# Attention units' scores and values set beside sample visits in a hybrid decoder step, with a later store and one subtraction moved between engines

## The chip, the cores and the metric

One core of a Trainium2 chip runs the whole step. The metric is the device time of one execution in microseconds. The engines are TensorE (PE in the profile; PEld is its loading of weights), VectorE (DVE), ScalarE (ACT), GpSimd (POOL) and SyncE (SP), which issues most of the DMAs. PE writes to PSUM, where an accumulator takes one of eight banks.

## The reference, cut to what matters

One layer of a decoder for a prompt of 1024 tokens and for 8 samples of 4 tokens, model width 1024. Two branches, each fed by the same projection, are joined by sigmoid gates:

```python
h, gate = adaln_in(x, c, w_ada, b_ada, g_norm)
(mq, mk, mv, mi, mf, mo, mz, aq, ak, av, az, gm, ga) = split_in(h @ w_in)
y_m, C, n, m = mlstm_branch(mq, mk, mv, mi, mf, mo, mz, C0, n0, m0, b_i, b_f, g_mn)
...
y_a = o.astype(x.dtype) * jax.nn.silu(az)          # o: sliding-window attention with sinks
u = jax.nn.sigmoid(gm) * (y_m @ w_mo) + jax.nn.sigmoid(ga) * (y_a @ w_ao)
x = x + gate * (u @ w_o)
```

The attention has 8 query heads in 2 groups of 64 channels and a window of 128 tokens: in blocks of 128 queries, scores against two blocks of keys, a softmax with a sink, and the values. The mLSTM branch goes through the prompt in chunks of 128 with a matrix memory per head; `m_p`, one of the outputs, is the last running maximum of its gates. The samples need the same projections, attention over a cache and an update of the matrix memories.

## The kernel before, in words

Nearly all of PE's time goes into the projections. A float32 product is made as three products of rounded parts (high times high, high times low, low times high). The first jobs are plain: 384 columns at a time, tiles `g_aq`, `g_mq` and so on. After the *plain jobs* come pairs of jobs as Strassen-like blocks (`block_products`, line 1698): seven products per pair, each of 12 matmuls of 512 columns, into the tiles `bx`, `bz`, `by` and `bw`. The attention's output projection has the same form (`AttPair` and `att_products`, lines 1840 and 1912; tiles `ax`, `az`, `ay`, `aw`).

All smaller work is put between these matmuls. `Side` (line 113) is the planner: it keeps a clock of its own, `side.now`, that each matmul advances by a modelled time, and streams of generators. A generator yields the time until its next step and the PSUM banks that the step needs (`a`, `b`, `o`; two of each). `tick` (line 140), called between matmuls, takes the steps that are due; a step that needs a bank only comes at a *visit*, when some time has passed since the last one (line 147). `HOLD` (line 110) says how long a step keeps a bank in this plan. PE's instructions stand in the order in which the program gives them; those of DVE and ACT are ordered by the framework's scheduler after the plain start, and each engine works through its own queue.

The streams that matter here:

- `unit(g, b0)` (line 931): one *attention unit*, two blocks of 128 queries of one group. It loads `uqk` and `uqv`, makes the scores (`sc`, in banks `o` behind the plain jobs, line 1166), their maxima and exponentials on DVE and ACT, the transposes of the probabilities (`pt`), and leaves its values to `values_now` (line 1013), which makes the tile `oT`, copies it to `p` on ACT and stores it to `oD` by POOL's queue. Before the change a unit that scores makes all waiting values first.
- `head(h)` (line 1181): an mLSTM head, with visits `tk`, `tv`, `S`, then `U`, `n`, and `ty`. `sample_head(h)` (line 1318): the samples of a head, with `stk`, `sS`, `sn`, `sU`, `st`, `sty`.
- *Sample visits*: once per pair, at the seventh or second block product, the samples' own projection is made from the raw weights: `samples_end` transposes the last pair's sums (`smpo`) and `samples` multiplies for the next pair (`smp`). Behind these the program calls `values_now` and a forced `tick` (lines 1781 and 1782). `smpo`, `smp` and `pt` use banks `b`.
- `gates` (line 668): the gates' maxima. Line 744 issues the store of `m_p` from `mn` as soon as the scan that makes `mn` is written. SP's queue is in order: a DMA that waits for its source holds those behind it. `store` and `due` (line 265) keep a store back until `side.now` has reached a given time.
- `AttPair.split` (line 1893): a weight block's high part is cast on ACT, its low part subtracted on DVE, except for blocks 3 and 4 of the first pair, which POOL subtracts (line 1902).

Of the kernel before, what the change touches and what calls it, by code (L numbers as in the profile page):

```python
# [10 lines left out]
F32 = mybir.dt.float32  # L11
# [4 lines left out]
ALU = mybir.AluOpType  # L16
# [90 lines left out]
JOBS = {n: i for i, n in enumerate(job_columns()[0])}  # L107


HOLD = {"a": 2.0, "b": 2.0, "o": 4.0, "+": 0.0}  # L110


class Side:
# [4 lines left out]
    def __init__(self, each, limits, quiet):  # L118
        self.each, self.free = each, {}
        self.now, self.last, self.quiet, self.products, self.left = 0.0, 0.0, quiet, 0, 99  # L120
        self.streams = {n: {"max": m, "gap": g, "wait": [], "live": [], "next": 0.0} for n, (m, g) in limits.items()}

    def add(self, stream, gen, banks=""):
# [16 lines left out]
    def tick(self, visit=False, then=None):  # L140
        self.each()
        for st in self.streams.values():
            if st["wait"] and len(st["live"]) < st["max"] and self.now >= st["next"]:
                self.begin(st)
        held, used = [], set()
        self.taken = False
        visit = visit or self.now >= self.last + self.quiet
        for item in sorted((i for st in self.streams.values() for i in st["live"]), key=lambda i: i[1]):
            banks = set(item[2])
            if self.now < item[1] or used & banks or (banks and not visit) or any(self.now < self.free.get(b, 0) for b in banks):  # L150
                continue
            used |= banks
            for b in banks:
                self.free[b] = self.now + (6.0 if "+" in banks else HOLD[b])
            if item[3]:
                held.append((item, self.now))
                self.now += 0.11 * item[3]
                continue
            n = self.products
            self.step(item)  # L160
            if self.products > n:
                self.last = self.now
        if then:
            then()
        now = self.now
        for item, self.now in held:
            self.step(item)
            self.last = max(self.last, self.now)
        self.now = now
# [17 lines left out]
def body(tc, a):  # L187
    nc = tc.nc
    with ExitStack() as ctx:
# [73 lines left out]
        due = []  # L263
# [404 lines left out]
        def gates(gp, zg, bias):  # L668
# [72 lines left out]
            V.tensor_tensor(d1, d1, bl, op=ALU.add)  # L741
            mn = cp.tile([1, 32], F32, name="mn")
            V.tensor_tensor_scan(mn, d0, d1, 0.0, ALU.add, ALU.max)
            dma(a["m_p"], mn.rearrange("p (h c) -> p h c", c=8)[:, :, 7])
            mr = cp.tile([1, 64], F32, name="mr")
            V.memset(mr[:, 32:33], 0.0)
            V.tensor_copy(mr[:, 33:64], mn[:, 0:31])
# [183 lines left out]
        def unit(g, b0):  # L931
            sink = at["sink"]
            los = [128 if b == 0 else 0 for b in (b0, b0 + 1)]
            n0 = 1 if b0 == 0 else 0
            qk, qv = ht([128, 4, 128], "uqk"), ht([128, 4, 128], "uqv")
            kT = qk[:, 1:4].rearrange("p c e -> p (c e)")
            q = qk[:, 0], qv[:, 0]
            vn = qv[:, 1], qv[:, 2], qv[:, 3]
            dma(kT[:, n0 * 128:], kD[:, (b0 - 1 + n0) * 128:(b0 + 2) * 128])
            for i in range(2):  # L940
                dma(q[i], qD[g][:, (b0 + i) * 128:(b0 + i + 1) * 128])
            dma(qv[:, 1 + n0:4], vnD[:, b0 - 1 + n0:b0 + 2])
            yield 12.0, sc_bank[1]
            values_now(pb if "+" in sc_bank[1] else po)
            p = [ht([128, 2, 256], f"p{kv}") for kv in range(2)]
            mx = sm([128, 4], "mx", 3)
            side.taken |= "+" in sc_bank[1]
            scs = [sc_bank[0]([128, 2, 256], f"sc{g}_{b0}_{kv}") for kv in range(2)]
            for i, lo in enumerate(los):
                kc = slice(i * 128 + lo, i * 128 + 256)  # L950
                for kv, r in enumerate(half_rows):
                    mm(scs[kv][:, i, lo:], q[i][r], kT[r, kc], start=True, stop=True, share=2)
            for kv in range(2):
                for i, lo in enumerate(los):
                    V.tensor_tensor_reduce(p[kv][:, i, lo:], scs[kv][:, i, lo:], amask[:, lo:], 1.0, sink[:, kv, g:g + 1],
                                           ALU.add, ALU.max, accum_out=mx[:, 2 * kv + i:2 * kv + i + 1])
            nmx = sm([128, 8], "nmx", 3)
            V.tensor_scalar(nmx[:, 0:4], mx, -1.0, None, op0=ALU.mult)
            v2 = lambda t: t.rearrange("p (k i) -> p k i", i=2)
            V.tensor_tensor(v2(nmx[:, 4:8]), sink[:, :, g:g + 1].to_broadcast((128, 2, 2)), v2(mx), op=ALU.subtract)  # L960
            yield 2.5, ""
            t0 = side.now
            yield from clear()
            den = sm([128, 4], "den", 3)
            S.activation(nmx[:, 4:8], nmx[:, 4:8], AF.Exp)
            for kv in range(2):
                for i, lo in enumerate(los):
                    j = 2 * kv + i
                    S.activation(p[kv][:, i, lo:], p[kv][:, i, lo:], AF.Exp, bias=nmx[:, j:j + 1],
                                 accum_out=den[:, j:j + 1])  # L970
            yield max(0.0, t0 + 3.0 - side.now), ""
            t0 = side.now
            yield from clear()
            V.tensor_tensor(den, den, nmx[:, 4:8], op=ALU.add)
            V.reciprocal(den, den)
            for kv in range(2):
                for i, lo in enumerate(los):
                    j = 2 * kv + i
                    if kv:
                        S.activation(p[kv][:, i, lo:], p[kv][:, i, lo:], AF.Copy, scale=den[:, j:j + 1])  # L980
                    else:
                        V.tensor_scalar(p[kv][:, i, lo:], p[kv][:, i, lo:], den[:, j:j + 1], None, op0=ALU.mult)
            yield max(0.0, t0 + 7.6 - side.now), "b", 2 * (4 - n0)
            pT = [t.rearrange("p i (j e) -> p (i j) e", e=128) for t in p]
            for kv in range(2):
                pt = (pb, pb if side.taken else po)[kv]([128, 4, 128], f"pt{g}_{b0}_{kv}")
                for j in range(n0, 4):
                    tr(pt[:, j], p[kv][:, j // 2, j % 2 * 128:j % 2 * 128 + 128], ident)
                if kv:
                    V.tensor_copy(pT[kv][:, n0:], pt[:, n0:])  # L990
                else:
                    S.copy(pT[kv][:, n0:], pt[:, n0:])
            yield 5.0, "o"
            due_values.append((g, b0, n0, vn, pT, p[0]))
            side.now = unit_products(n0)
            side.products += 2 * (4 - n0)
            units_done.append((g, b0))
# [15 lines left out]
        def values_now(pool=po):  # L1013
            joins_now()
            was, n = side.now, side.products
            side.taken |= pool is po and len(due_values) > 0
            for g, b0, n0, vn, pT, home in due_values:
                oT = pool([128, 2, 128], f"oT{g}_{b0}")
                for j in range(n0, 4):
                    i, hf = divmod(j, 2)  # L1020
                    for kv in range(2):
                        r = slice(64 * kv, 64 * kv + 64)
                        mm(oT[r, i], vn[i + hf][:, r], pT[kv][:, j], start=(hf == 0 or b0 + i == 0), stop=(hf == 1))
                c0 = b0 * 128
                o = home[:, 0]
                S.copy(o, oT.rearrange("p c e -> p (c e)"))
                issue(oD[g][:, c0:c0 + 256], o, eng=nc.gpsimd)
            due_values.clear()
            side.now, side.products = was, n

        def queries(g):
# [111 lines left out]
        def head_jobs(h):  # L1143
# [15 lines left out]
            for n, dst, smp, scale in (("mq", q, qs, float(128 ** -0.5)), ("mk", k, ks, 1.0), ("mv", v, vs, 1.0)):  # L1159
# [3 lines left out]
                if i == -1:  # L1163
                    plain_ends.append(True)
                    side.finish("g")
                    sc_bank[:] = po, "o+"
                    side.streams["a"]["max"] = 3
                    next(work)
                job((n, h), keep(dst, smp, scale, "s"), (lambda: next(work)) if i == -1 else None)
# [11 lines left out]
        def head(h):  # L1181
# [128 lines left out]
            if h == 2:  # L1310
                at["n0"], at["n1"] = (cp.tile([128, NH, NB], F32, name=n) for n in ("n0", "n1"))
                dma(at["n0"], a["state_n"])
                for i in range(NH):
                    side.add("s", sample_head(i), "ob")

        tails = []

        def sample_head(h):
            an, sxb, fls, wes = st["an"], st["sxb"], st["fls"], st["wes"]
            z = ht([128, 512], "sz")  # L1320
            kn = sm([96, 128], "skn", 1, F32R)
# [55 lines left out]
                    G.tensor_scalar(c, c, sxb[:, h, 2, b:b + 1], None, op0=ALU.mult)  # L1377

            joins.append(states)
            yield 4.0, "o"  # L1380
            settle(states)
            yield 4.0, "ob"
            for i, (c, b, m) in enumerate(zip(Cs, bs, ns_)):
# [314 lines left out]
        def block_products(jobs, hook):  # L1698
# [27 lines left out]
            for j, (n, i) in enumerate(flat):  # L1726
# [45 lines left out]
                if i == (2 if n else 7) and nxt:  # L1772
# [4 lines left out]
                        side.now += nxt.cost  # L1777
                    else:
                        nxt.samples()
                    values_now()  # L1780
                    side.free["b"] = side.now + HOLD["b"]
                    side.tick(True, values_now)
                    if nxt.kind in (head_in, gate):
                        nxt.first_sums()
                if i == 7 and nxt and nxt.kind not in (head_in, gate):
# [54 lines left out]
        class AttPair:  # L1840
# [52 lines left out]
            def split(self, i):  # L1893
# [5 lines left out]
                hi, lo = self.w[i] = [x[:, o:o + 2] for x in self.g[home]]  # L1899
                with behind(S, self.landed if i == 1 else []):  # L1900
                    S.copy(hi, t)
                (G if (self.i, i) in ((0, 3), (0, 4)) else V).tensor_tensor(lo, t, hi.bitcast(F32), op=ALU.subtract)
                if i == 2:
                    V.tensor_tensor(r0[:, 2:4], r0[:, 2:4], r0[:, 0:2], op=ALU.subtract)

# [757 lines left out]
```

## Time and profile before

| | us |
| --- | --- |
| time, three runs | 811.42, 811.79, 813.1 (median 811.79) |
| the profiled execution: its time, its span | 811.34, 809.6 |
| busy PE, PEld | 796.6, 668.8 |
| busy DVE, ACT, POOL | 600.7, 418.5, 82.3 |

The span goes from the first to the last instruction. The granted clock of TensorE is 0.999 over the span. In the profile's lines a row of the timeline reads: start, duration, engine, line, operation, out<-in, shape, count, and in brackets the idle time ahead with what ended it. A matmul's duration reaches past the start of the next, since they are pipelined; the distance between two starts is the time that one costs. Each float32 matmul of a visit leaves two records.

### The profile page before, as it was taken

The page shows a single profiled execution, that of the slowest core. Times are in us where ns is not written, and L with a number is a line of the kernel's source. Part 1 is how long each engine was busy: PE and PEld are TensorE (multiplying, and loading weights), DVE is VectorE, ACT ScalarE, POOL GpSimd, SP SyncE. Part 2 cuts the span into 40 slices and gives each one's busy share as a digit, 9 for nine tenths or more (in the row PEclk, how much of TensorE's full clock was granted, in tenths as well). Part 3 has the DMA queues.
Part 4 walks back from the last instruction along what each step waited for, and adds up shares of the span by engine and source line. Part 5 has one row for each costly group of instructions (what it writes and reads, how often), then busy time and mean ns, then how long its engine had stood idle before and what let it go on. Part 6 is the DMA issues. An engine that isn't in the chain of part 4 may idle for free.

```text
span 809.6 us, 15159 instructions
## 1 busy us (share of the span) xinstructions
PE 796.6 (98%) x5156; PEld 668.8 (83%) x5156; DVE 600.7 (74%) x1499; ACT 418.5 (52%) x1019; POOL 82.3 (10%) x158
## 2 busy tenths in 40 slices
PE   8999999999999999999999999999999999999996
PEld 5779888998788888888888888888888779996785
DVE  4899997647656466476657888998678998865776
ACT  5664346656474574556556655554446552224335
POOL 0120000010000000000001441330003201000000
PEclk9999999999999999999999999999999999999999
DMA  9994855556545425537655695675246599649322
GB/s 348 362 352 154 262 176 178 184 177 212 157 150 171 139 85 163 192 101 255 244 191 182 240 278 208 226 253 171 83 156 211 164 302 390 220 164 335 124 105 111
DMA packets 113794, 165.51 MB, mean 204 GB/s; under 512 B 21248, under 2 KB 55936, under 8 KB 113684
## 3 DMA queue, kind: packets, MB, share of 16 engines
q1 hardware_dynamic: 107316, 152.21, 56.9%
q10 hardware_dynamic: 4752, 7.60, 2.5%
q0 software_dynamic: 1648, 4.72, 1.5%
q8 instruction: 41, 0.67, 0.3%
q14 instruction: 37, 0.30, 0.1%
HBM read 115.51 MB, written 50.00 MB: 204 GB/s over the span
## 4 chain that ended last, share of the span: by engine, by line
PE 89%; DVE 5%; DMA 3%; issue 1%; ACT 1%; SPq 0%; DVEq 0%; ACTq 0%
PE by L296 13%; PE bw L296 12%; PE bx L296 12%; PE bz L296 6%; PE g_w_mo L296 6%; PE g_mq L296 3%; PE foW L296 3%; PE foY L296 2%; PE foX L296 2%; PE smp L296 2%; PE oT L296 2%; PE n L296 2%; PE g_ak L296 2%; PE sc L296 2%; PE pt L301 1%; PE g_mk L296 1%
## 5 line engine op out<-in xcount | busy, mean ns | idle before, releaser
L233 DVE CUSTOM_DVE_ANT_0 p<-sc,cst,sink 128x256 f32<-128x256 f32 (+1 forms) x64 | 26.3, 462 | 12.3 <-PE sc L296 11.1
L233 ACT ACTIVATE p<-p,nmx 128x256 f32<-128x256 f32 (+1 forms) x64 | 30.9, 484 | 8.3 <-DVE nmx L233 8.3
L233 POOL TENSOR_SCALAR Cs<-Cs,sxb 128x129 f32<-128x129 f32 x32 | 29.2, 930 | 45.7 <-PE sn L296 45.7
L296 PE MATMUL g_aq<-h_h,wh_aq 128*128 128x384 f32 (+1 forms) x96 | 31.9, 332 | 0.0
L296 PE MATMUL g_aq<-h_h,wl_aq 128*128 128x384 f32 (+1 forms) x96 | 30.9, 321 | 0.0
L296 PE MATMUL g_aq<-h_l,wh_aq 128*128 128x384 f32 (+1 forms) x96 | 30.8, 321 | 0.0
L296 PE MATMUL g_w_mo<-ym_h,wh_w_mo 128*128 128x384 f32 (+1 forms) x96 | 30.8, 321 | 0.0
L296 PE MATMUL g_w_mo<-ym_l,wl_w_mo 128*128 128x384 f32 (+1 forms) x96 | 30.8, 321 | 0.0
L296 PE MATMUL g_w_mo<-ym_l,wh_w_mo 128*128 128x384 f32 (+1 forms) x96 | 30.8, 321 | 0.0
L233 ACT CAST wosh<-wor 128x512 fp32r<-128x512 f32 x24 | 14.8, 622 | 13.8 <-DVE wor L233 13.8
L282 POOL DMA_DIRECT2D oD<-p x16 | 8.7, 544 | 130.1 <-ACT p L233 120.3
L233 DVE TENSOR_TENSOR wosl<-wor,wosh 128x512 fp32r<-128x512 f32 x24 | 16.7, 695 | 3.4 <-ACT wosh L233 2.6
L233 DVE COPY p<-pt 128x512 f32<-128x512 f32 (+1 forms) x16 | 10.5, 654 | 11.7 <-PE pt L301 11.6
L296 PEld LDWEIGHTS g_aq<-h_h,wh_aq 128*128 128x128 f32 x96 | 18.0, 188 | 1.0 <-issue 1.0
L233 DVE SCALAR_TENSOR_TENSOR tgw_mo<-tgw_mo,g_w_mo 128x384 f32<-128x384 f32 (+1 forms) x24 | 12.4, 518 | 8.1 <-PE g_w_mo L296 7.3
L296 PEld LDWEIGHTS g_w_mo<-ym_l,wl_w_mo 128*128 128x128 f32 x96 | 18.0, 188 | 0.1
L296 PEld LDWEIGHTS g_w_mo<-ym_l,wh_w_mo 128*128 128x128 f32 x96 | 18.0, 188 | 0.0
L296 PEld LDWEIGHTS g_aq<-h_l,wh_aq 128*128 128x128 f32 x96 | 18.0, 188 | 0.0
L296 PEld LDWEIGHTS g_w_mo<-ym_h,wh_w_mo 128*128 128x128 f32 x96 | 18.0, 188 | 0.0
L296 PEld LDWEIGHTS g_aq<-h_h,wl_aq 128*128 128x128 f32 x96 | 18.0, 188 | 0.0
L233 DVE TENSOR_TENSOR et<-et,S 128x384 f32<-128x384 f32 (+1 forms) x12 | 6.1, 510 | 15.8 <-PE S L296 15.8
L233 ACT ACTIVATE p<-p,den 128x256 f32<-128x256 f32 (+1 forms) x32 | 14.8, 491 | 3.8 <-DVE dec L233 2.1
(2072 smaller groups left out, 2837.7 us busy)
## 6 DMA issues: line engine op xcount, KB each, us to landing
early_h<-w_ada SPq DMA_DIRECT2D x8, 512.0 KB
adar_ga<-w_ada SPq DMA_DIRECT2D x16, 256.0 KB
wr_ga<-w SPq DMA_DIRECT2D x16, 256.0 KB
wr_gm<-w SPq DMA_DIRECT2D x16, 256.0 KB
taD<-gt SPq DMA_DIRECT2D x16, 256.0 KB
tmD<-gt SPq DMA_DIRECT2D x16, 256.0 KB
wor<-w_out SPq DMA_DIRECT2D x16, 256.0 KB
tga<-taD SPq DMA_DIRECT2D x16, 256.0 KB
```

Source lines behind the costliest of these rows:

```text
L233: ins = f(*args, **kw)
L282: ins = (eng or nc.sync).dma_start(out, in_)
L296: in_order(nc.tensor.matmul(out, lhsT, rhs, start=start, stop=stop, skip_group_check=more))
L301: in_order(nc.tensor.transpose(out, in_, idn))
```

## The change

It has three parts.

*Units and sample visits.* Behind the plain jobs a unit's scores now ask for a bank `!`, which `tick` gives only while `side.beside` is set, that is in the forced tick of a sample visit; they also must be free 3.5 us ahead by the plan. Values of at most two units at a time are made, into one tile, behind the scores of the same visit (in banks `b`) or, where there are none, as before in a bank `o`. Sample heads begin 8 to 17 us behind a sample visit, and their state products wait for the next one for up to 20 us. As the order of PE stands, PE has the same 3863 rows in all.

*The store of `m_p`* becomes due 14 us later on the planner's clock.

*Block 3 of the first attention pair* is subtracted on DVE instead of POOL.

```diff
-HOLD = {"a": 2.0, "b": 2.0, "o": 4.0, "+": 0.0}
+HOLD = {"a": 2.0, "b": 2.0, "o": 4.0, "+": 0.0, "!": 0.0}
...
+        self.beside, self.scored, self.turn = False, False, 0.0
...
-            if self.now < item[1] or used & banks or (banks and not visit) or any(self.now < self.free.get(b, 0) for b in banks):
+            if "!" in banks and not self.beside:
+                continue
+            now = self.now + 3.5 * ("!" in banks)
+            if now < item[1] or used & banks or (banks and not visit) or any(now < self.free.get(b, 0) for b in banks):
                 continue
...
-            dma(a["m_p"], mn.rearrange("p (h c) -> p h c", c=8)[:, :, 7])
+            due.append((side.now + 14.0, a["m_p"], mn.rearrange("p (h c) -> p h c", c=8)[:, :, 7]))
...
             yield 12.0, sc_bank[1]
-            values_now(pb if "+" in sc_bank[1] else po)
+            if not side.beside:
+                values_now(pb if "+" in sc_bank[1] else po)
...
+            side.scored = True
...
-            for g, b0, n0, vn, pT, home in due_values:
-                oT = pool([128, 2, 128], f"oT{g}_{b0}")
+            now = due_values[:2]
+            both = pool([128, 4, 128], f"oT{now[0][0]}_{now[0][1]}") if now else None
+            for x, (g, b0, n0, vn, pT, home) in enumerate(now):
+                oT = both[:, 2 * x:2 * x + 2]
...
-            due_values.clear()
+            del due_values[:2]
...
-                    sc_bank[:] = po, "o+"
+                    sc_bank[:] = po, "o+!"
...
-                    side.add("s", sample_head(i), "ob")
+                    side.add("s", sample_head(i))
...
+            while not 8.0 <= side.now - side.turn <= 17.0 and side.now < side.turn + 40.0:
+                yield 0.3, ""
+            yield 0.0, "ob"
...
-            yield 4.0, "o"
+            t0 = side.now
+            yield 4.0, ""
+            while states in joins and side.now < t0 + 20.0:
+                yield 0.5, ""
+            if states in joins:
+                yield 0.0, "o"
             settle(states)
...
-                    values_now()
+                    joins_now()
                     side.free["b"] = side.now + HOLD["b"]
-                    side.tick(True, values_now)
+                    side.beside, side.scored = True, False
+                    side.tick(True, lambda: values_now(pb if side.scored else po))
+                    side.beside, side.turn = False, side.now
...
-                (G if (self.i, i) in ((0, 3), (0, 4)) else V).tensor_tensor(lo, t, hi.bitcast(F32), op=ALU.subtract)
+                (G if (self.i, i) == (0, 4) else V).tensor_tensor(lo, t, hi.bitcast(F32), op=ALU.subtract)
```

Below, the new lines' numbers are a few higher than the old ones'. On PE, the scores of the unit of group 3 at block 2 (`sc_2`) stand before the change by themselves between two block products, `bz` and `bw`:

```order
L296 MATMUL bz<-h_l_401,wh_phead_in_5__3005 128x512
L296 MATMUL bz<-h_h_400,wl_phead_in_5__3006 128x512
L296 MATMUL sc_2_0_3145<-uqk 128x256
L296 MATMUL sc_2_1_3146<-uqk 128x256
L296 MATMUL sc_2_0_3145<-uqk,uqv 128x256
L296 MATMUL sc_2_1_3146<-uqk,uqv 128x256
L296 MATMUL bw<-t2h_889,wh_phead_in_6__3032 128x512
L296 MATMUL bw<-t2l_890,wh_phead_in_6__3032 128x512
```

With the change they stand behind the last products of a sample visit (`smp`), and the values of an earlier unit (`oT_6`, eight products of which two are shown) stand behind them:

```order
L300 MATMUL smp<-wr_mk_1_3335,c_102 32x128
L300 MATMUL smp<-wr_mv_0_3337,c_102 32x128
L300 MATMUL smp<-wr_mv_1_3339,c_102 32x128
L300 MATMUL sc_2_0_3492<-uqk 128x256
L300 MATMUL sc_2_1_3493<-uqk 128x256
L300 MATMUL sc_2_0_3492<-uqk,uqv 128x256
L300 MATMUL sc_2_1_3493<-uqk,uqv 128x256
L300 MATMUL oT_6_3505<-p_2884,uqv 64x128
L300 MATMUL oT_6_3505<-p_2885,uqv 64x128
```

Five units have moved so, one to each of five sample visits in a row; counting each stretch of other products between two rows of projections as a visit, PE has 104 visits where it had 110. Two visits of transposes (`pt`) now stand right behind a `U`, one behind an `n`.

On DVE, at the start of the attention's output projection, before (`wl_ao0C` is the low part of blocks 7 and 3 of the first pair, `u_h<-tga,ax` empties the bank of `ax`):

```order
L233 TENSOR_TENSOR wl_ao0C<-wr_ao_7583,wh_ao0C 128x256
L233 TENSOR_TENSOR ws_7868<-wr_ao_7481 128x256
L233 TENSOR_TENSOR wr_ao_7481<-wr_ao_7480,wr_ao_7481 128x256
L233 TENSOR_TENSOR wl_ao1A<-wr_ao_7480,wh_ao1A 128x256
L233 TENSOR_TENSOR wr_ao_7480<-ws_7868,wr_ao_7480 128x256
L233 SCALAR_TENSOR_TENSOR u_h_7780<-tga,ax 128x512
L233 TENSOR_REDUCE smps<-smpo 128x256
```

and with the change:

```order
L237 TENSOR_TENSOR wl_ao0C<-wr_ao_7581,wh_ao0C 128x256
L237 TENSOR_TENSOR ws_7866<-wr_ao_7479 128x256
L237 TENSOR_TENSOR wr_ao_7479<-wr_ao_7478,wr_ao_7479 128x256
L237 TENSOR_TENSOR wl_ao1A<-wr_ao_7478,wh_ao1A 128x256
L237 TENSOR_TENSOR wl_ao0C<-wr_ao_7580,wh_ao0C 128x256
L237 SCALAR_TENSOR_TENSOR u_h_7778<-tga,ax 128x512
L237 TENSOR_REDUCE smps<-smpo 128x256
```

The second `wl_ao0C` has come from POOL, and the second `wr_ao` has gone behind `u_h`: the number of instructions ahead of `u_h` is the same.

On SP, before, the store of `m_p` stands ahead of weight loads, a unit's loads and the stores of `qD`:

```order
L282 DMA adar_ga_1389<-w_ada 128x512
L282 DMA m_p<-mn 4x1x1
L282 DMA adar_ga_1407<-w_ada 128x512
L282 DMA gbD<-gb_1148 1x512
L282 DMA adar_ga_1448<-w_ada 128x512
L282 DMA uqk<-kD 128x384
```

and with the change it stands 18 DMAs later, by the order's own numbers, next to the store of `nmd`:

```order
L286 DMA qD_116<-aqr 128x384
L286 DMA qD_116<-aqr 128x256
L286 DMA nmd<-gt_854 32x128
L286 DMA m_p<-mn 4x1x1
L286 DMA qD_117<-aqr 128x384
L286 DMA wr_mv_0_1666<-w 128x512
```

It has passed the loads and stores between, and now has one `qD` store and the loads of `wr_mv` behind it.

## The prediction

> **What bounds the kernel now.** I read the page first: the shares of the engines and the chain that ended last. Then the busy time by stretch, the timeline of TensorE at the places that the change touches, and the waits there.
>
> ```profile
> span 809.6 us, 15159 instructions
> PE 796.6 (98%) x5156; PEld 668.8 (83%) x5156; DVE 600.7 (74%) x1499; ACT 418.5 (52%) x1019; POOL 82.3 (10%) x158
> PE 89%; DVE 5%; DMA 3%; issue 1%; ACT 1%; SPq 0%; DVEq 0%; ACTq 0%
> ```
>
> TensorE (PE) is busy for 796.6 of 809.6 us and has 89% of the chain. Time can fall only where PE stands still, or where it spends time that is no product. By stretch (the columns are busy time and instructions of PE, PEld, DVE, ACT, POOL, then clock, DMA share, GB/s):
>
> ```profile
> 198.00:330.00 132.00, 132.00 (x912) 108.63 (x912) 79.17 (x215) 75.03 (x208) 6.91 (x17) 1.00 0.46 144
> 618.00:660.00 42.00, 40.79 (x235) 32.70 (x233) 41.14 (x84) 24.77 (x57) 6.76 (x5) 1.00 0.69 224
> ```
>
> From 198 to 330 us lie the attention units that the change moves. PE never idles there at a clock of 1.00, while VectorE (DVE) has 53 us free: no wait is there to remove. From 618 to 660 us it is the other way: DVE is busy for 41.14 of 42 us, and PE loses 1.2 us.
>
> **The visits (five scores beside sample visits).** The long stream of 512-column products is broken by visits: transposes, scores, values. What a break costs beside its own products is read from the start times of the products around it. A visit of one unit's scores alone:
>
> ```profile
> 234.64 0.39 PE L296 MATMUL bz<-h_l,wh_phead_in__3005 128*128 128x512 f32 x1
> 234.87 0.40 PE L296 MATMUL bz<-h_h,wl_phead_in__3006 128*128 128x512 f32 x1
> 235.20 0.70 PE L296 MATMUL sc<-uqk 64*128 64x256 f32 x4
> ...
> 236.26 0.50 PE L296 MATMUL bw<-t2h,wh_phead_in__3032 128*128 128x512 f32 x1
> 236.60 0.39 PE L296 MATMUL bw<-t2l,wh_phead_in__3032 128*128 128x512 f32 x1
> ```
>
> Two products of the stream start 0.23 us apart (234.64, 234.87). The scores start 0.33 after the last of them, so 0.10 is lost on entering; the second product behind them starts 0.34 after the first, so 0.11 on resuming: 0.21 in all, beside 1.06 of scores. A visit that begins with transposes, of 128 by 128:
>
> ```profile
> 238.22 0.40 PE L296 MATMUL bw<-t2h,wl_phead_in__3033 128*128 128x512 f32 x1
> 238.45 0.82 PE L301 MATMUL pt<-cst,p 128*128 128x128 f32 x6
> 239.03 0.48 PE L296 MATMUL bw<-t2h,wh_phead_in__3032 128*128 128x512 f32 x1
> 239.34 0.39 PE L296 MATMUL bw<-t2l,wh_phead_in__3032 128*128 128x512 f32 x1
> ```
>
> It enters at 0.23, so free, and resumes at 0.31: 0.08 in all. And the sample visit, with values behind it:
>
> ```profile
> 242.55 0.27 PE L301 MATMUL smpo<-cst,smps 128*128 128x128 f32 x1
> 242.75 0.30 PE L296 MATMUL smp<-wr_mv,c 128*32 128x128 f32 x2
> ...
> 243.76 1.09 PE L296 MATMUL oT<-p,uqv 128*64 128x128 f32 x16
> 244.78 0.50 PE L296 MATMUL by<-t3h,wh_phead_in__3158 128*128 128x512 f32 x1
> 245.12 0.39 PE L296 MATMUL by<-t3l,wh_phead_in__3158 128*128 128x512 f32 x1
> ```
>
> The order of PE has as many products as before. Five visits that begin with scores or values are gone, their products standing in sample visits: 5 x 0.21 = 1.05. Two visits of transposes join a U visit and one joins an n visit, against one that had ridden behind scores and one n that had ridden behind values, so one cheap visit less, 0.08. That makes six visits fewer and 1.1 us. How scores fare right behind smp is shown nowhere before; the nearest row is values behind smp, which leave at 0.11 as after any other visit. Ends: 1.3, were all six to count 0.21; 0.6, were scores in each of the five to pay an entry of 0.10 inside the visit. I take 1.1, as values behind smp are the nearest case.
>
> The Trainium skill ("TensorEngine Tiling (Array Packing)", Key Properties) says that a change of tiling mode drains TensorE. That speaks against the gain: apart, sample visit and scores with values change mode five times, together still four (32 columns, 64 rows, 64 columns, full). By it one drain per visit is saved; at the 0.10 of the scores' entry, 0.5 us in place of 1.05. The trace agrees in that 64-row scores pay 0.10 on entering and full transposes nothing; it does not show that resuming costs by mode, since transposes pay 0.08 there too.
>
> **One subtraction from GpSimd to VectorE.** The only stop of PE after the start above 1 us:
>
> ```profile
> 638.95 0.40 PE L296 MATMUL ay<-yat3h,wl_ao0C 128*128 128x512 f32 x1
> 640.55 0.47 PE L296 MATMUL ax<-ym_l,wh_ao1A 128*128 128x512 f32 x1 [1.21 <-DVE u_h L233]
> ```
>
> The new ax needs the bank that DVE empties in u_h<-tga,ax. Ahead of that on DVE, and on GpSimd (POOL) at the same time:
>
> ```profile
> 637.59 0.88 DVE L233 TENSOR_TENSOR wr_ao<-wr_ao,wr_ao 128x256 f32<-128x256 f32 x1
> 638.39 0.96 DVE L233 TENSOR_TENSOR wl_ao1A<-wr_ao,wh_ao1A 128x256 fp32r<-128x256 f32 x1
> 639.38 0.42 DVE L233 TENSOR_TENSOR wr_ao<-ws,wr_ao 128x256 f32<-128x256 f32 x1
> 639.73 0.68 DVE L233 SCALAR_TENSOR_TENSOR u_h<-tga,ax 128x512 f32<-128x512 f32 x1
> 637.45 0.73 POOL L233 TENSOR_TENSOR wl_ao0C<-wr_ao,wh_ao0C 128x256 fp32r<-128x256 f32 x1 [1.85 <-ACT wh_ao0C L233]
> 638.15 0.92 POOL L233 TENSOR_TENSOR wl_ao0D<-wr_ao,wh_ao0D 128x256 fp32r<-128x256 f32 x1
> ```
>
> The same kind of instruction takes 0.42 alone and 0.88 and 0.96 while POOL works: it ends just behind POOL's. By starts the two take 0.80 and 0.99 against 0.35 (639.38 to 639.73), so 1.1 is lost to the two POOL instructions. After the change POOL has one; DVE has wl_ao0C in front of u_h, but a wr_ao goes behind u_h in exchange, so the count ahead stays. Half of 1.1 goes: 0.6, and PE waits 0.6 instead of 1.2. Ends: 0, if the one left still holds up both; 1.2, if it falls where DVE is not hurt. I take 0.6, one of two alike. What is late next is the rest of this same wait.
>
> **The store of the maxima.** SP's queue, and the two rows that it can reach:
>
> ```profile
> 99.10 0.85 SPq L282 DMA_DIRECT2D adar_ga<-w_ada  x2
> 108.27 0.62 SPq L282 DMA_DIRECT2D m_p<-mn  x1
> 116.93 1.16 SPq L282 DMA_DIRECT2D qD<-aqr  x2
> 119.60 0.49 ACT L233 ACTIVATE aq<-g_aq 128x384 f32<-128x384 f32 x1 [0.40 <-DMA qD<-aqr]
> 120.14 0.44 PE L296 MATMUL g_mq<-h_h,wh_mq 128*128 128x384 f32 x1 [0.56 <-ACT aq L233]
> ```
>
> The queue stands from 99.95 to 108.27 for mn, and everything behind it (two weight loads, a unit's four loads, then the stores of qD) is issued late. ACT waits 0.40 for such a store to land, and PE 0.56 for ACT. Issued behind nmd, m_p finds mn long made and holds nobody, but takes its own slot of up to 0.62 ahead of qD's third store. Ends: 0.4 gained, 0.2 lost; I take 0.2 gained, as ACT's 0.40 is the only row that hangs on it and other waits of SP's queue may hold the qD stores as long.
>
> The rest is free while its covers hold: values of two units in one bank are the same products; sample heads begin 8 to 17 us behind a sample visit, and the units' softmax runs elsewhere than before, under a DVE that is free for 53 of 132 us. Without that cover each late evacuation would be a wait on PE, up to the 0.88 or so of one DVE instruction that it stands behind.
>
> **The sum.** 1.1 + 0.6 + 0.2 = 1.9 us. The profiled execution took 811.34 (span 809.6 and 1.7 around it), 0.45 below the median of 811.79. So 809.4 for such an execution, and 809.9 for the median. 0.2%, 1.6 us, is about what a measurement of this kernel can tell from no change.
>
> **Rivals.**
> - *Each change of shape costs, wherever it stands.* If what a break costs hangs on changes of the products' shape at 0.10 each, a merged visit has one change less than the two apart, and saves 5 x 0.10 = 0.5. The sum is 0.5 + 0.1 + 0.6 + 0.2 = 1.4, so 810.4; with nothing from the last two, 811.2. For it: the 0.10 at the scores' entry, where transposes pay none. Against: values behind smp leave at 0.11, as scores alone do. That is the drain rule of the Trainium skill's page on tiling, above. Chance 0.16.
> - *The wait at 640 stays.* POOL's remaining instruction still lands on DVE's critical pair, or the added one on DVE takes back what is won. 809.9 + 0.6 = 810.5. For it: DVE is full from 618 to 660. Against: equal counts ahead of u_h. Chance 0.12.
> - *Slower: values wait for a bank.* In a merged visit values take the bank that smpo had, which DVE must first empty by its reduction. From smpo to values lie 0.20 + 1.01 (242.55 to 243.76) + 1.06 = 2.27 us.
>
> ```profile
> 242.86 0.29 DVE L233 TENSOR_REDUCE smps<-smpo 128x64 f32<-128x128 f32 x1 [0.77 <-PE smpo L301]
> 449.23 0.27 PE L301 MATMUL smpo<-cst,smps 128*128 128x128 f32 x1
> 453.44 0.28 DVE L233 TENSOR_REDUCE smps<-smpo 128x64 f32<-128x128 f32 x1
> ```
>
> At 242 the reduction ends 0.60 after smpo starts, at 449 4.49. It decides once the lag passes 2.27; at 4.49 a visit loses 2.2 us, and at the middle, two of the five, 809.9 + 4.4 = 814.3. Against: DVE waited 0.77 for smpo at 242, so it was not behind. Chance 0.12.
>
> My forecast has 0.60, with its own range from 808.9 to 810.8: 1.3 + 1.2 + 0.4 = 2.9 at most, 0.6 + 0.3 + 0.1 = 1.0 at least, as the ends at nothing are the rivals'. I put three quarters of it under 810.2. So faster 0.60 x 0.75 + some 0.05 of the first two rivals = 0.50; slower by 0.2% (above 813.4) 0.09, most of the third; 0.41 between. The range for 8 in 10 runs from 808.8 to 812.2: down to the highest gain, up over both mild rivals and one such wait (809.9 + 2.2 = 812.1).
>
> **What would show it.** Five visits smpo, smp, sc, oT between 214 and 335 us, with sc starting within 0.1 of smp's end and the product after oT resuming at 0.34; no PE wait from 198 to 515 us; SP issuing m_p without a pause and no gap of 8 us at 100; one POOL subtraction at 638, and 0.6 instead of 1.2 us of idle PE ahead of ax. A PE wait on smps, n or pt in the moved stretch, or oT held behind DVE, would make the forecast wrong.

## The result: slower by 1.2 us, and where it went

| | median, us | ratio to before, 95% interval |
| --- | --- | --- |
| before | 811.79 | |
| after | 812.98 | 1.0015 (1.0008 to 1.0022) |
| after, measured a second time | 812.83 | 1.0014 (1.0005 to 1.0024) |

The forecast was 809.9, with a range from 808.8 to 812.2; the measured 812.98 lies above it. The change costs 1.2 us where 1.9 were to be gained. It stays within the 0.2% that I called the measurable, but with 21 runs a side its sign is clear. The page of after, its shares and its chain:

```profile
span 811.7 us, 15166 instructions
PE 798.2 (98%) x5156; PEld 669.8 (83%) x5156; DVE 600.6 (74%) x1500; ACT 418.6 (52%) x1019; POOL 80.3 (10%) x157
...
PE 89%; DMA 4%; DVE 3%; ACT 2%; issue 1%; SPq 0%; ACTq 0%; DVEq 0%
```

The shares are nearly those of before. By stretch, in the columns of the prediction's table:

```profile
198.00:330.00 132.00, 131.53 (x884) 109.24 (x884) 79.21 (x214) 73.50 (x203) 5.80 (x15) 1.00 0.45 143
618.00:660.00 42.00, 41.38 (x237) 33.30 (x236) 41.44 (x85) 24.68 (x58) 5.97 (x4) 1.00 0.69 215
```

PE, which never idled from 198 to 330 us, now does for 0.47; at 640 it lost 1.2 and loses 0.6. To see the rest I laid the two traces over each other at the main products, which come in the same order in both, and read the start times: how far after lies behind before at each place, and where that changes. I did it with the first two profiles and again with a second profile of each kernel, since the execution that the first profile of after shows took 813.5, 0.5 above its median.

| stretch, us | what lies there | forecast | first pair | second pair |
| --- | --- | --- | --- | --- |
| 0 to 60 | first loads land | 0 | -0.35 | -0.19 |
| 117 to 128 | `g_mq` behind the `qD` store | -0.2 | -0.73 | -0.28 |
| 160 to 175 | values of two units | 0 | +0.32 | +0.36 |
| 197 to 508 | the visits | -1.1 | +2.18 | +2.02 |
| 633 to 646 | `ax` behind `u_h` | -0.6 | -0.60 | -0.57 |
| 733 to 745 | `fo` waits for `w_out` from DRAM | 0 | +1.34 | -0.04 |
| sum | with crumbs elsewhere | -1.9 | +2.16 | +1.41 |

The second pair adds up to about what the medians say. The 1.34 at the end is a matter of the single execution: from the last product ahead of `fo` to the first one behind it are 4.54 us in the first profile of before and 5.38 in the second, 5.87 and 5.34 in the two of after. What stays is the stretch of the visits. PE's list of waits over the whole span of after (time in all, times, longest):

```profile
PE oT L300 <- ACT p L237: 0.9, 2, 0.5
PE ty L305 <- DVE et L237: 0.7, 1, 0.7
...
PE ax L300 <- DVE u_h L237: 0.6, 1, 0.6
...
PE smp L300 <- ACT p L237: 0.2, 1, 0.2
...
PE smp L300 <- ACT hk L237: 0.2, 1, 0.2
```

Before, the same list has `ax` with 1.2 and `g_mq` with 0.6, and neither `oT` nor `ty`. The two new waits in the timeline: first a merged sample visit with the values of two units.

```profile
210.90 0.27 PE L305 MATMUL smpo<-cst,smps 128*128 128x128 f32 x1
...
212.11 0.70 PE L300 MATMUL sc<-uqk 64*128 64x256 f32 x4
...
213.17 0.88 PE L300 MATMUL oT<-p,uqv 128*64 128x128 f32 x12
...
214.10 0.37 ACT L237 COPY p<-oT 128x256 f32<-128x256 f32 x1 [1.32 <-PE oT L300]
...
214.52 1.09 PE L300 MATMUL oT<-p,uqv 128*64 128x128 f32 x16 [0.47 <-ACT p L237]
215.55 0.50 PE L300 MATMUL bx<-h_h,wh_phead_in__2816 128*128 128x512 f32 x1
```

The first unit's twelve products need about 0.7 us from 213.17; then PE stands until ACT has copied them out (214.10 plus 0.37), and only then makes the second unit's sixteen. The two units share one tile, and the copy of the first stands between their products. From the first product to the stream's next are 2.38 us; with a tile for each unit (own_banks, below) they are 1.68, so this visit loses 0.7. The visit of two units at 165 us waits as long, but there the second unit's products began 0.32 late before the change as well, in a tile of their own, so the change costs 0.32 to 0.36. Next the transposes `ty` of the third prompt head, and VectorE's chain of 8-column instructions that they wait for:

```profile
424.20 0.30 DVE L237 SCALAR_TENSOR_TENSOR f8den<-et 128x3 f32<-128x3 f32 x3
...
424.70 0.16 DVE L237 TENSOR_TENSOR f8den<-f8den,fl 128x8 f32<-128x8 f32 x1
424.77 0.69 DVE L237 TENSOR_TENSOR wor<-wor,wor 128x512 f32<-128x512 f32 x1
425.38 0.20 DVE L237 RECIPROCAL f8den<-f8den 128x8 f32<-128x8 f32 x1
...
432.78 0.39 PE L300 MATMUL bw<-h_h,wl_pgate__5314 128*128 128x512 f32 x1
...
433.38 2.15 DVE L237 TENSOR_SCALAR et<-et,f8den,f8r_y 128x128 f32<-128x128 f32 x8
...
433.88 2.04 PE L305 MATMUL ty<-cst,et 128*128 128x128 f32 x8 [0.71 <-DVE et L237]
...
435.67 0.48 PE L300 MATMUL bw<-h_h,wh_pgate__5313 128*128 128x512 f32 x1
```

Each of the chain's instructions takes 0.16 to 0.20 us, but VectorE's queue has one of 0.69 between most of them, so the chain takes from 424.20 to 433.38, when the eight scalings of `et` begin. PE reaches `ty` 0.23 after 432.78, starts it at 433.88 (0.87 late), and the eight transposes, paced by the eight scalings, take 1.79 to the next product instead of 0.79: 1.9 us in all, of which the list shows 0.7. Before the change the chain ran from 422.51 to 428.52, with fewer instructions between its own, and the scalings were done 2.2 us ahead of `ty`:

```profile
428.52 2.14 DVE L233 TENSOR_SCALAR et<-et,f8den,f8r_y 128x128 f32<-128x128 f32 x8
...
432.88 1.03 PE L301 MATMUL ty<-cst,et 128*128 128x128 f32 x8
433.67 0.48 PE L296 MATMUL bw<-h_h,wh_pgate__5315 128*128 128x512 f32 x1
```

What went as forecast, in after: a merged visit without a wait; the subtraction; and the store.

```profile
238.81 0.27 PE L305 MATMUL smpo<-cst,smps 128*128 128x128 f32 x1
...
239.81 0.28 PE L300 MATMUL smp<-wr_mq,c 128*32 128x128 f32 x2
240.02 0.49 PE L300 MATMUL sc<-uqk 64*128 64x128 f32 x4
...
240.88 1.09 PE L300 MATMUL oT<-p,uqv 128*64 128x128 f32 x16
241.90 0.50 PE L300 MATMUL by<-t3h,wh_phead_in__3121 128*128 128x512 f32 x1
242.24 0.39 PE L300 MATMUL by<-t3l,wh_phead_in__3121 128*128 128x512 f32 x1
```

From `smpo` to `by` are 3.09 us. Apart, the sample visit takes 1.21 and such scores with values 1.88: the same 3.09. It resumes at 0.34. So one break is gone and nothing is paid inside.

```profile
639.17 0.85 POOL L237 TENSOR_TENSOR wl_ao0D<-wr_ao,wh_ao0D 128x256 fp32r<-128x256 f32 x1 [2.15 <-ACT wh_ao0D L237]
...
639.34 0.96 DVE L237 TENSOR_TENSOR wl_ao1A<-wr_ao,wh_ao1A 128x256 fp32r<-128x256 f32 x1
640.22 0.41 DVE L237 TENSOR_TENSOR wl_ao0C<-wr_ao,wh_ao0C 128x256 fp32r<-128x256 f32 x1
640.56 0.67 DVE L237 SCALAR_TENSOR_TENSOR u_h<-tga,ax 128x512 f32<-128x512 f32 x1
...
641.38 0.47 PE L300 MATMUL ax<-ym_l,wh_ao1A 128*128 128x512 f32 x1 [0.62 <-DVE u_h L237]
```

One GpSimd instruction is left, one VectorE instruction of 0.96 beside it, and `ax` waits 0.62 instead of 1.21. On SP's queue there is no gap of 8 us any more, and `m_p` takes its slot ahead of `qD`'s third store:

```profile
103.79 3.91 SPq L286 DMA_DIRECT2D adar_ga<-w_ada  x3
...
114.21 0.39 SPq L286 DMA_DIRECT2D nmd<-gt  x1
114.64 0.64 SPq L286 DMA_DIRECT2D m_p<-mn  x1
115.75 0.33 SPq L286 DMA_DIRECT2D qD<-aqr  x1
```

### The profile page after: what moved, and what is told of

The parts are those of the page before. It is cut to its first block, busy times and chain, and to the rows that moved or that the text cites. A ratio compares the mean times of both kernels' runs of the same rounds, so it can differ in the third digit from the quotient of the medians.

```text
span 811.7 us, 15166 instructions
## 1 busy us (share of the span) xinstructions
PE 798.2 (98%) x5156; PEld 669.8 (83%) x5156; DVE 600.6 (74%) x1500; ACT 418.6 (52%) x1019; POOL 80.3 (10%) x157
## 4 chain that ended last, share of the span: by engine, by line
PE 89%; DMA 4%; DVE 3%; ACT 2%; issue 1%; SPq 0%; ACTq 0%; DVEq 0%
PE by L300 12%; PE bw L300 12%; PE bx L300 12%; PE bz L300 6%; PE g_aq L300 6%; PE g_w_mo L300 5%; PE g_mq L300 3%; PE smp L300 2%; PE foY L300 2%; PE sc L300 2%; PE foW L300 2%; PE oT L300 2%; PE foX L300 2%; PE pt L305 2%; PE n L300 1%; PE g_mk L300 1%
## 5 line engine op out<-in xcount | busy, mean ns | idle before, releaser
L300 PE MATMUL oT<-p,uqv 128*64 128x128 f32 x240 | 16.6, 279 | 0.9 <-ACT p L237 0.9
L300 PEld LDWEIGHTS oT<-p,uqv 128*64 128x64 f32 x240 | 12.8, 136 | 5.1 <-ACT p L237 1.4
```

The source lines that it names most:

```text
L300: in_order(nc.tensor.matmul(out, lhsT, rhs, start=start, stop=stop, skip_group_check=more))
```

## The experiments

The theory: the visits save what was priced, and the shared tile and the chain ahead of `ty` take back more than that. The rivals: what is won early is lost again at the end of the kernel, where `fo` waits for its weights; or merged visits save nothing, because a change of shape is paid wherever it stands. Ratios are to the kernel before, timed beside each kernel on the same chip. Many of the intervals overlap, so most differences between two kernels of this table rest on start times too.

| kernel | median, us | ratio, 95% interval |
| --- | --- | --- |
| small_only | 810.51 | 0.9989 (0.9980 to 0.9998) |
| store_only | 810.95 | 0.9995 (0.9986 to 1.0004) |
| no_pool | 810.18 | 0.9985 (0.9976 to 0.9994) |
| visits_only | 813.87 | 1.0026 (1.0016 to 1.0037) |
| copies_last | 811.82 | 1.0004 (0.9995 to 1.0013) |
| own_banks | 811.89 | 1.0005 (0.9997 to 1.0014) |
| ty_early | 810.75 | 0.9990 (0.9981 to 0.9999) |
| both_fixed | 809.70 | 0.9978 (0.9969 to 0.9987) |
| split_visits | 812.59 | 1.0013 (1.0004 to 1.0022) |
| best_all | 809.31 | 0.9976 (0.9967 to 0.9986) |

**The parts taken apart.** small_only is before with the two small parts, visits_only after without them, store_only before with the later store alone.

```diff
-            dma(a["m_p"], mn.rearrange("p (h c) -> p h c", c=8)[:, :, 7])
+            due.append((side.now + 14.0, a["m_p"], mn.rearrange("p (h c) -> p h c", c=8)[:, :, 7]))
...
-                (G if (self.i, i) in ((0, 3), (0, 4)) else V).tensor_tensor(lo, t, hi.bitcast(F32), op=ALU.subtract)
+                (G if (self.i, i) == (0, 4) else V).tensor_tensor(lo, t, hi.bitcast(F32), op=ALU.subtract)
```

> The kernel before with the two small parts of the change alone: the store of m_p due 14 later, block 3 of the first attention pair subtracted on VectorE; units and sample visits as before. Theory (the visits' new waits are the whole loss): the store keeps the 0.7 us by which the profiles of before and after part at 118 to 127 us, the subtraction the 0.6 at 635 to 644, so 1.3 us faster than before, 810.5, ratio 0.9984. Rival (what is won ahead of the last stage is lost there again, since the sample rows' products fo at 735 to 745 wait for their weights to land, whenever the products before them end): within 0.3 us of before, ratio 1.000, and a longer wait of fo in the profile.

> The changed kernel with the two small parts undone: the visits' part of the change alone. Theory: the difference of the medians is 1.2 us, of which the small parts make -1.3, so the visits alone make the kernel 2.5 us slower, 814.3, ratio 1.0031; in the profile ty near 433 stands again some 1.9 us and a two-unit oT half a microsecond. Rival: the small parts are worth nothing at the end, so 1.2 slower, 813.0, ratio 1.0015.

> The kernel before with the store of m_p due 14 later, nothing else. Theory: g_mq's wait of 0.56 for ACT's aq goes and 0.7 us with it, 810.8, ratio 0.9991; the gain stands from 120 us to the end. Rival (what I had forecast): 0.2 us, 811.3, ratio 0.9998.

The small parts make the kernel faster by 0.11% (0.9 us), the visits slower by 0.26% (2.1 us); together 1.2, as after has it. The tail does not swallow what is won: the rival's ratio of 1.000 for small_only lies outside the interval, if only just, and by start times small_only ends 1.28 and 1.42 us ahead of the two profiles of before. The store's size stays uncertain, because the wait that it removes differs between executions. At 117 to 128 us the eleven profiles with the later store all lie 0.71 to 0.77 ahead of the first profile of before; the two others with the early store, visits_only and the second profile of before, lie 0.25 and 0.48 ahead of it, and in the latter PE's list has no wait for `aq` at all. So the later store gains 0.2 to 0.8 by the execution that it is held against. The time of store_only, 0.05% less, does not differ from none, and does not decide between my 0.2 and the 0.7 that I expected here from one profile.

**Copies behind the products.** The edit to after, with PE's order unchanged:

```diff
                         mm(oT[r, i], vn[i + hf][:, r], pT[kv][:, j], start=(hf == 0 or b0 + i == 0), stop=(hf == 1))
+            for x, (g, b0, n0, vn, pT, home) in enumerate(now):
                 c0 = b0 * 128
                 o = home[:, 0]
-                S.copy(o, oT.rearrange("p c e -> p (c e)"))
+                S.copy(o, both[:, 2 * x:2 * x + 2].rearrange("p c e -> p (c e)"))
```

> The changed kernel; where the values of two units share a tile, both units' products are written ahead of both copies, so that no product stands behind a copy of the same tile. PE's order of instructions is the same. Theory: the two waits of oT for ACT's p (0.9 us in the list of waits, 0.32 + 0.53 by start times) go: 0.8 us faster than the changed kernel, 812.2, and no oT <- ACT p among PE's waits. Rival (the tail sets the end): the waits go and the time stays, 813.0.

The same visit, PE's and ACT's rows on `oT`:

```profile
212.61 1.75 PE L300 MATMUL oT<-p,uqv 128*64 128x128 f32 x28
...
214.40 0.65 ACT L237 COPY p<-oT 128x256 f32<-128x256 f32 x2 [2.19 <-PE oT L300]
```

All 28 products in one run, the copies behind them, no wait: 1.0004 instead of 1.0015, some 0.9 to 1.2 us. By start times 0.73 come from this visit and 0.66 to 0.69 from the one at 165 us; of the latter, 0.33 is the delay that the kernel before had there too. own_banks gives each unit a tile of its own and leaves the copies where they were:

```diff
-            both = pool([128, 4, 128], f"oT{now[0][0]}_{now[0][1]}") if now else None
...
-                oT = both[:, 2 * x:2 * x + 2]
+                oT = pool([128, 2, 128], f"oT{g}_{b0}")
```

> The changed kernel with a tile of its own for each unit's values, as before the change, copies between the units as in the change. Theory (the wait is for the copy of the shared tile): oT no longer waits for ACT's p; but in the sample visit near 211 the second unit's tile is the bank of smp, which ACT copies behind its start (0.27 at 212.51), long ahead of oT: no wait, 1.1 faster than the changed kernel, as with the copies last: 811.9. Rival (the bank of smp is free only late): oT waits for smps instead, 812.5 to 813.

Again no `oT` in the list of waits and the same time (811.89 beside 811.82): the wait is one for the shared tile. At 211 us the second tile finds its bank free (1.68 us, as in copies_last); at 165 its products begin 0.32 late, as before the change, which the list does not show. The Trainium skill ("PSUM — Partial Sum Buffer", PSUM bank collisions raise a hardware error) says that TensorE's writes and another engine's reads of one bank in the same 32 partitions have to be kept apart, even where they touch other columns. The trace agrees as far as it goes: the two units write different columns of one tile, and PE waits for the copy (0.47 at 214.52). Whether the program waits because of the tile or because of the bank these runs do not tell apart, and what would happen without the wait was not tried.

**The factors earlier.** For the third prompt head the steps of the chain are written two microseconds sooner; `ty` stays where it was.

```diff
-                          [(stage_c, 2), 5.0, ""], [(stage_f, 0), 4.0, ""], [(stage_c3, 0), (stage_c3, 1), (stage_c3, 2), 6.0, "ob"],
+                          [(stage_c, 2), 3.0 if h == 2 else 5.0, ""], [(stage_f, 0), 6.0 if h == 2 else 4.0, ""], [(stage_c3, 0), (stage_c3, 1), (stage_c3, 2), 6.0, "ob"],
```

> The changed kernel; the factors of the third prompt head (the chain of small f8 instructions on VectorE) are written 2 us earlier on the planner's clock, everything else at the same time: PE's order is unchanged, on VectorE the chain stands ahead of the state updates and subtractions that it was mixed with. Theory: ty near 433 no longer waits for et, 1.9 us faster than the changed kernel, 811.1; if the subtractions behind the chain now come late, 0.6 of it is taken back by a wait on their product (one VectorE instruction of 0.68). Rival (the tail sets the end): 813.0.

```profile
416.36 0.47 DVE L237 SCALAR_TENSOR_TENSOR f8den<-et 128x3 f32<-128x3 f32 x3
416.86 0.17 DVE L237 TENSOR_TENSOR f8den<-f8den,fl 128x8 f32<-128x8 f32 x1
...
421.20 1.12 DVE L237 TENSOR_SCALAR et<-et,f8den,f8r_y 128x128 f32<-128x128 f32 x4
...
433.12 1.03 PE L305 MATMUL ty<-cst,et 128*128 128x128 f32 x8
433.91 0.48 PE L300 MATMUL bw<-h_h,wh_pgate__5313 128*128 128x512 f32 x1
```

The chain runs from 416.36 to 421.20, 4.8 us instead of 9.2, and `ty` enters on time and takes 0.79. The kernel is 2.0 to 2.2 us faster than after (0.9990 against 1.0014 and 1.0015), and no product behind the chain waits. Here the chain could begin 7.8 us earlier than in after, with PE's order unchanged: in after it was late by its place in the queue.

**Both, and the price of a break.** both_fixed has both edits. split_visits starts from it and makes what stood behind `smp` three products ahead of the sample visit, as a visit of its own.

```diff
                     mm(o, wl[:, k], bh, start=False, stop=(k == 3), more=not new)
+                    if k == 2 and i == (2 if n else 7) and nxt:
+                        was = side.now
+                        side.now += 1.9
+                        side.beside, side.scored = True, False
+                        side.tick(True, lambda: values_now(pb if side.scored else po))
+                        side.beside = False
+                        later.append(side.now - was - 1.9)
+                        side.now = was
+                        continue
...
-                    side.beside, side.scored = True, False
-                    side.tick(True, lambda: values_now(pb if side.scored else po))
-                    side.beside, side.turn = False, side.now
+                    side.now += later.pop()
+                    side.turn = side.now
```

> The changed kernel with both repairs together: copies behind both units' products, and the third prompt head's factors written earlier. Theory (the visits save what was priced, and two waits gave it back): the two earlier gains add up, 1.1 + 2.2 off the changed kernel: 809.7, ratio to before 0.998, and less than the two small parts alone (810.5) by what the visits save net of the small waits that stay, some 0.7. Rival (merged visits save nothing, their breaks are paid inside): no faster than the two small parts alone, 810.5, ratio 0.999.

> The kernel with both repairs, in which what stands behind smp in a sample visit (scores with values, U with values, values, sn) is made three products of the stream ahead of the sample visit instead: 104 visits become 114, the visits between stay nearly as they were. Theory (a break costs 0.10 on entering and 0.11 on resuming): 10 x 0.21 = 2.1 us slower than with both repairs, 811.8. Rival (a change of shape costs 0.10 wherever it stands: scores and values have one change less behind smp than apart): 10 x 0.10 = 1.0 slower, 810.7. Second rival (a break is free beside its waits): 809.7. Waits that the new order brings would come on top, and are read from the list of waits.

both_fixed came out at 809.70 as expected, 0.8 to 0.9 less than the small parts alone. Not all of that is the merging: by start times both_fixed gains 0.54 on small_only from 197 to 508 us, and 0.37 at 165, where the copies behind the products remove a delay that the kernel before had too. So merged visits do pay once their waits are gone, but 0.5 us. In split_visits the visit of 238.81 above has become two:

```profile
237.12 0.39 PE L300 MATMUL bx<-h_h,wl_phead_in__3070 128*128 128x512 f32 x1
237.44 0.49 PE L300 MATMUL sc<-uqk 64*128 64x128 f32 x4
...
239.32 0.50 PE L300 MATMUL bx<-h_h,wh_phead_in__3069 128*128 128x512 f32 x1
239.66 0.40 PE L300 MATMUL bx<-h_l,wh_phead_in__3069 128*128 128x512 f32 x1
...
321.73 0.48 PE L300 MATMUL sc<-uqk 64*128 64x256 f32 x1 [1.43 <-DVE et L237]
```

The scores enter 0.32 after the last product and the stream resumes at 0.34, so 0.09 and 0.11. Added up over all visits from 190 to 520 us (the distance on entering and the one on resuming, each less the stream's 0.227), breaks cost 4.97 us in 53 visits of both_fixed and 6.73 in 61 of split_visits: 1.76 for 8. Of the ten visits split off nine cost 0.20 or 0.21, as priced, and the one that begins with `U` 0.11; two visits of transposes are joined to others and save 0.09 each. The time rose by 0.35% (2.8 us), more than the theory's 2.1. The new order also brought a wait of scores for VectorE (the last row; that visit is 2.1 longer). The profiled execution took 814.35, 1.8 above this kernel's median, so how much of that wait a usual one has is not known, and the time alone would not decide. The start times do, against the rival's 0.10. The Trainium skill's rule that a change of tiling mode drains TensorE ("TensorEngine Tiling (Array Packing)", Key Properties) would count one change per split visit: the rows show twice the 0.10 that a change costs on entering, because the way back into the stream costs as much.

**No subtraction on GpSimd.** no_pool is small_only with block 4 on VectorE too, where the order puts it behind `u_h`.

```diff
-                (G if (self.i, i) == (0, 4) else V).tensor_tensor(lo, t, hi.bitcast(F32), op=ALU.subtract)
+                V.tensor_tensor(lo, t, hi.bitcast(F32), op=ALU.subtract)
```

> The kernel with the two small parts, in which block 4 of the first attention pair is subtracted on VectorE too, so GpSimd does nothing near 638. On VectorE that subtraction stands behind u_h<-tga,ax, so what is ahead of u_h is the same. Theory (each GpSimd instruction holds up the VectorE instruction beside it by half a microsecond): wl_ao1A takes 0.42 instead of 0.96 and ax waits about 0.1 instead of 0.6: 0.5 faster than with the two small parts, 810.0. Rival (VectorE was simply full there): ax waits 0.6 as before and later evacuations stand 0.35 later, 810.5 to 810.9.

```profile
636.83 0.42 DVE L233 TENSOR_TENSOR wl_ao1A<-wr_ao,wh_ao1A 128x256 fp32r<-128x256 f32 x1
...
637.50 0.68 DVE L233 SCALAR_TENSOR_TENSOR u_h<-tga,ax 128x512 f32<-128x512 f32 x1
...
638.33 0.47 PE L296 MATMUL ax<-ym_l,wh_ao1A 128*128 128x512 f32 x1
...
641.53 0.47 PE L296 MATMUL ay<-yat4h,wh_ao0D 128*128 128x512 f32 x1 [0.22 <-DVE u_h L233]
```

`wl_ao1A` takes 0.42, not 0.96, and `ax` is no longer in the list; a new wait of 0.22 stands at `ay`, whose bank VectorE empties later. So of the 0.6 that small_only left, 0.24 is gained by start times; the medians differ by 0.3, which is within the intervals.

**Everything together, and second profiles.** best_all is both_fixed with no_pool's line.

> The kernel with both repairs, and with block 4 of the first attention pair subtracted on VectorE too. Theory: the gains are in different stretches and add up: both repairs 809.7, the block 0.3 (810.51 to 810.18): 809.4, ratio 0.9975. Rival (transfers at the end take back what is won): 809.7.

> The changed kernel a second time. Theory: the 1.3 us by which the two profiles part at 735 to 745, where the sample rows' products fo wait for their weights from DRAM, is a matter of the single execution (other kernels of this study showed 0.1 to 1.1 there): another amount now, and 1.0015 of before's time. Rival: the part belongs to the change: 1.3 again.

> The kernel before a second time, for its profile. Theory: at 735 to 745 it parts from its first profile by something between 0 and 1.3 us, as the single execution has it. Rival: by less than 0.1.

809.31 is the fastest of all: 0.24% less than before, 0.39% less than after. Its margin over both_fixed (0.4) is within the intervals. The last two are the second pair of the table at the head: at 733 to 745 before differs from itself by 0.85, and after, the other way, by 0.5; the rival, that this part belongs to the change, falls.

## Why the prediction was wrong, point by point

- *Visits, -1.1 at 0.21 a break.* The price was right: 0.20 or 0.21 a break in split_visits, and from 198 to 508 us the breaks cost 5.95 us in 58 visits of small_only and 4.85 in 52 of both_fixed, 1.1 saved. What I took from it, that the stretch gets shorter by that much, was not: the breaks' -1.1, 0.7 of longer visits, 1.1 of waits for the copy and 1.9 at `ty` make +2.6, where the table has 2.4 to 2.5 from 160 to 508 us.
- *"The rest is free while its covers hold."* This is the step that failed, in both halves. "Values of two units in one bank are the same products" is true and beside the point: the same products in one tile, with a copy written between them, wait for that copy. It cost 0.32 to 0.36 at 165 us and 0.7 at 214, about 1.1 together; copies_last takes 0.9 to 1.2 off the time. I read the order of PE's instructions and not that of the copies between them.
- *"Under a DVE that is free for 53 of 132 us."* A free share says nothing of a chain of sixteen dependent small instructions that VectorE's queue mixes with others of 0.69. In the first profile of before the scalings ended at 430.66, 2.2 us ahead of `ty`; after, the new order of the queue ended it 2.5 us behind (433.38 + 2.15 against 433.01). That cost 1.9 us by start times, 2.0 to 2.2 by ty_early. I had bounded a late evacuation by the 0.88 of one VectorE instruction; here a whole chain was late, in a stretch of the kernel (432 us) far behind the units that were moved. That it comes with the moved visits is shown by visits_only, which has the same wait of 0.7 on its list; why the framework's scheduler placed the chain so stays open.
- *The smaller rest.* both_fixed still gains only 0.54 from 197 to 508 where the breaks save 1.1: the visits' own products take 0.7 longer (71.71 us instead of 71.04 in small_only), among them `smp` behind ACT's `hk` (0.27 by start times), values behind U (0.17) and transposes behind U or n (0.08 to 0.09 each, as much as a break of theirs costs, so that joining those gains nearly nothing).
- *Subtraction, -0.6.* Right in size and mechanism: 0.60 and 0.57, and in no_pool, with the second instruction gone from GpSimd, the rest of the wait of `ax` is gone.
- *Store, -0.2.* 0.73 in the first pair, 0.28 in the second, 0.05% in time: not wrong, and not settled between these, since the wait that it removes was itself 0.2 to 0.8 long.
- *Rivals.* The change of shape that costs wherever it stands is refuted by split_visits; the wait at 640 was halved as forecast. The slower rival named values waiting for `smpo`'s bank, which happened nowhere. The loss came from a wait of its kind, a product behind an evacuation, at two places that I had not named. Of my signs, "no PE wait from 198 to 515 us" caught them, with `oT` at 214, `smp` at 399 and `ty` at 434; the ones that name a cause ("smps, n or pt", "oT held behind DVE") did not: `oT` was held behind ACT, and `ty` was not named.

## What to carry to other kernels

Merging visits of a matmul stream gains the price of a break each, which can be read off start times; but list for every merged piece what evacuates its bank and where that evacuation is written, since products that share a tile wait for each other's copies. When PE's order is changed, follow every chain of small dependent instructions on the other engines to the product that needs its end, over the whole stretch and not only where the edit is. And take a second profile of each kernel before putting a difference of half a microsecond down to the change.

## What the runs showed of the hardware

Two-input VectorE subtractions of 128x256 take 0.42 us alone and 0.84 to 0.97 when they begin while a GpSimd subtraction of the same kind is under way: in the twelve profiles with such an instruction on GpSimd they ended 0.28 behind it at each of sixteen meetings. One that was already under way when GpSimd's began kept its 0.42, and with none on GpSimd all took 0.41 to 0.43. The Trainium skill ("SBUF — State Buffer", Who interferes with whom) has the two engines hold a shared pair of ports for a whole instruction, so that the later one waits: VectorE's 0.96 in after began 0.17 after GpSimd's 0.85 and ended 0.28 behind it, which agrees. And executions of one and the same kernel differ at a few places, `fo`'s weights from DRAM by up to 0.85 us, `g_mq` by 0.5, `g_ak` at 52 us by 0.25 and one visit at 322 us by 0.2, while past the first 11 us the stream's products between these places keep their distance to a few hundredths.
